# Turned edge blocks of the bands in unused scores columns, two PSUM banks each for middles and sums

## The chip, the core and the metric

The kernel runs on one core of one Trainium2 chip. The metric is device time in microseconds (us) of one launch. Five engines run side by side, each in the order of its own instruction list: TensorE (PE in the profile; its weight loads are listed apart as PEld), VectorE (DVE), ScalarE (ACT), GpSimd (POOL) and SyncE (SP, which issues the DMAs). They hold each other up only through semaphores. TensorE writes its results into PSUM, which has 8 banks; a bank holds 512 fp32 values in each of the 128 partitions. VectorE and ScalarE read them from there.

## What is computed

A two-layer encoder trunk over 1024 tokens of width 1024. In each layer a normalised and modulated input goes through one projection, whose columns feed three groups of attention heads; their outputs are normalised by group, joined, projected back and added to the input; a SwiGLU block follows. Cut to what matters here:

```python
ya = neighborhood_attention(qa, ka, va, rpb_na[l])                  # 4 heads
yb = sliding_window_attention(qb, kb, vb, sink_sw[l], t5_table)     # 6 heads
yc = axial_attention(qc, kc, vc, gq_ax[l], gk_ax[l])                # 6 heads, dense
y = concatenate([rms_norm(ya, ga), rms_norm(yb, gb), rms_norm(yc, gc)], axis=-1)
x = x + gt_a * (y @ w_o[l])
```

For the first two kinds a block of 128 queries sees only three blocks of 128 keys: its own, the one before and the one after. The kernel calls such heads bands (A: the neighbourhood, B: the sliding window).

## The kernel before

**The stream.** The attention of a layer is a list of 64 pairs. A pair is two neighbouring query blocks of one head, so a head has four pairs (p = 0 to 3). Pairs 0 to 23 are the six dense heads (C), 24 to 39 the four heads of A, 40 to 63 the six heads of B. One loop walks over n; in step n work of several pairs is issued, so that each engine finds something ready. While `pin` is on, TensorE, ScalarE and VectorE run in exactly the order in which the code issues. What stands outside (statistics and scales of the group norms, splits of `y` and of weights, the first matmuls of the output projection) is placed freely by a scheduler.

**A step of the bands (n from 24 on), as written.**

1. `divide` for pair n+2: VectorE reciprocal, POOL scales both halves of the probabilities `pr`.
2. `low` for pair n-1: VectorE subtracts the rounded copy from the turned block, `pt<-T` on DVE.
3. `combine` for pair n-3 if its p is odd: VectorE adds the two halves of the head, `y<-pv,cmb`.
4. `scores` for pair n+4: four matmuls into a scores tile (`sA` or `sB`, two banks, columns 0 to 383 of each used), then two VectorE instructions, here called the mins, that add the bias, write `pr` and give the row's extreme.
5. `exps` for pair n+3: two ScalarE exponentials with sums.
6. `turn` for pair n: TensorE transposes the four middle blocks into a tile `T` (`t_tile`, one bank) and the one or two edge blocks (the key blocks outside the pair's own two) into a second such tile `E`, named `T` too in the profile. ScalarE copies both out: `pt<-T` and `edge<-T`.
7. `pv` for pair n-2: four matmuls with the middles, one or two with the edges, into half of a sums bank `pv`; two pairs share a bank.
8. `fold` for pair n-2 if p is odd: ScalarE copies one half, `cmb<-pv`.

**PSUM.** The scores pool `psS` has two tiles of two banks. The remaining four banks are a pool `psT` of three (`PS_T = 3`), from which `T`, `E` and the tiles of the norm statistics (`ps_st`, `ps_r`) are taken in turn, and a pool `psV` of one bank for the sums:

```python
psT_cm, psT = open_pool("psT", bufs=PS_T, space=PSUM)
psV_cm, psV = open_pool("psV", bufs=4 - PS_T, space=PSUM)
```

With one sums bank, the `pv` of an even pair (step n) has to wait for `combine` of the pair before it, which is issued in the same step. `E` of pair n takes the bank that `T` of pair n-1 held, so its transposes wait for `low` of pair n-1, also of the same step.

**After the bands.** From n = 60 no scores are left to issue; the scheduler then places matmuls of the output projection (`ps_o`) between the last turns and sums, with weights split by ScalarE (`whi`) and VectorE (`wlo`).

Of the kernel before, what the change touches and what calls it, by code (L numbers as in the profile page):

```python
# [19 lines left out]
P = 128  # L20
# [7 lines left out]
EPS = 1e-6  # L28
MASKED = 1e30
BIG = 3.0e38  # L30
PS_T = 3

# [53 lines left out]
def trunk(ctx: ExitStack, tc, A, C, out):  # L86
# [19 lines left out]
    def close(cm):  # L106
        cm.__exit__(None, None, None)
# [153 lines left out]
    class Ahead:  # L261


        def __init__(self, gen):
            self.gen, self.have = gen, []
# [592 lines left out]
    for l in range(2):  # L858
# [446 lines left out]
        ap_cm, app = open_pool("apad", side="right")  # L1305
        pad(app, 32)
        at_cm, atp = open_pool("att", side="right")
        psT_cm, psT = open_pool("psT", bufs=PS_T, space=PSUM)
        psV_cm, psV = open_pool("psV", bufs=4 - PS_T, space=PSUM)

        def zA_tile():
            return atp.tile([P, 640], F32, name="zA", tag="zA", bufs=2)
# [19 lines left out]
        def rs_tile():  # L1332
            return atp.tile([P, 8], F32, name="rs", tag="rs", bufs=6)

        def t_tile():
            return psT.tile([P, 4, P], F32, name="T", tag="T")

        def split_pt(T, hi, lo):
            act.copy(hi, T)
# [2 lines left out]
        class Pair:  # L1342

            by_columns = False

            def __init__(self, row, vh, p):
                self.row, self.vh, self.p = row, vh, p
# [9 lines left out]
            def products(self, movs, part):  # L1359
                if part == 0:  # L1360
                    if self.p % 2 == 0:
                        open_pv[0] = psV.tile([P, H], F32, name="pv", tag="V")
                    self.pvt = open_pv[0]
                c0 = (self.p % 2) * 256
                half = (len(movs) + 1) // 2
                for n, (kc, at, mvs) in enumerate(movs):
                    if (n < half) != (part == 0):
                        continue
                    for i, mv in enumerate(mvs):
                        v = vs[:, kc, self.vh, :]  # L1370
# [51 lines left out]
        class PairC(Pair):  # L1422
# [21 lines left out]
            def turn_high(self, c, kb):  # L1444
                if c == kb == 0:
                    self.pt = [[pt_tile() for _ in range(2)] for _ in range(2)]
                cc = slice(c * P, (c + 1) * P)
                T = t_tile()
# [59 lines left out]
        class Band(Pair):  # L1508


            def __init__(self, row, vh, p, q, k, sk=None):
# [7 lines left out]
            def scores(self):  # L1519
                rs, p, sk = self.rs, self.p, self.sk  # L1520
                s, pr = psS.tile([P, 2, 512], F32, name=self.name, tag="S"), self.pr
                for c, (a, b) in enumerate(self.spans):
                    j = 2 * p + c
                    for i in range(2):
                        pe.matmul(
                            s[:, c, a:b], self.q[:, j * P : (j + 1) * P],
                            self.k[i][:, (j - 1) * P + a : (j - 1) * P + b],
                            start=(i == 0), stop=(i == 1),
                        )
                for c, (a, b) in enumerate(self.spans):  # L1530
# [17 lines left out]
            def divide(self):  # L1548
                divide([self.pr[:, c, a:b] for c, (a, b) in enumerate(self.spans)], self.rs)

            def turn(self):
                pr = self.pr
                T, self.pt = t_tile(), [pt_tile() for _ in range(2)]
                for b in range(2):
                    for i in range(2):
                        pe.transpose(
                            T[:, 2 * b + i, :], pr[:, b, (1 - b + i) * P : (2 - b + i) * P], ident
                        )
                edges = [pr[:, 0, 0:P]] * self.left + [pr[:, 1, 2 * P : 3 * P]] * self.right
                E = t_tile()  # L1560
                for i, src in enumerate(edges):
                    pe.transpose(E[:, i, :], src, ident)
                hi, lo = (
                    t[:, 0:2, :].rearrange("p i (c q) -> p c i q", c=2) for t in self.pt
                )
                T = T.rearrange("p (c i) q -> p c i q", c=2)
                act.copy(hi, T)
                e = self.e = atp.tile([P, 2, P], F32, name="edge", tag="edge", bufs=3)
                act.copy(e[:, 0 : len(edges)], E[:, 0 : len(edges)])
                self.low = lambda: sub(lo, T, f32(hi))  # L1570

            def pv(self):
# [142 lines left out]
        for n in range(-AHEAD - 1, N + 3):  # L1715
            ahead = AHEAD if n + AHEAD < NC else AHEAD_B
            begin = range(done, min(n + ahead + 1, N))
            if n < 0:
                begin = range(done, done)
            elif n == 0:  # L1720
                opened(*(pairs[i] for i in range(4)))
                begin = range(3, 4)
                fresh = []
            elif n < NC:
                for i in range(2 if n > 1 else 0):
                    if 0 <= n:
                        pairs[n].turn(i)
                    while unfinished:
                        unfinished.pop(0)()
                    if 2 <= n - 1:  # L1730
                        pairs[n - 1].pv(i)
                    for m in begin:
                        if m < min(made, NC):
                            pairs[m].qk(i)
                for i in range(2 if n == 1 else 0):
                    pairs[begin[0]].qk(i)
                fresh = [pairs[m] for m in begin if NC <= m < made]
                for b in fresh:
                    b.scores()
                    b.exps()  # L1740
                    b.divide()
            else:
                for b in worked:
                    b.divide()
                if NC <= n - 1 < N:
                    pairs[n - 1].low()
                if NC <= n - 3:
                    pairs[n - 3].combine()
                fresh = [pairs[m] for m in begin if m < made]
                for b in fresh:  # L1750
                    b.scores()
                for b in scored:
                    b.exps()
                if n < N:
                    pairs[n].turn()
                if NC <= n - 2 < N:
                    pairs[n - 2].pv()
                    pairs[n - 2].fold()
                elif n == NC:
                    for i in range(2):  # L1760
                        pairs[n - 1].pv(i)
                scored, worked = fresh, scored
# [37 lines left out]
            for end, (chunks, width) in norms.items():  # L1800
                if begins[end] <= m <= end and (m - begins[end]) % 8 == 7 and (n <= NC or m >= NC):
# [9 lines left out]
                    if m == end and end < N - 1:  # L1811

                        def stats(end=end, width=width, n=n, chunks=chunks):
                            r = rstd_cols([gss[end]], width, 8, atp, psT, tag="T", newton=True)

                            def scale():
                                todo = norm_scale(chunks, r, psT, "T", (pool, pool))
# [8 lines left out]
        close(psV_cm)  # L1826
        close(psT_cm)
        close(vs_cm)


# [694 lines left out]
```

## Time and profile before

| | |
|---|---|
| median of 3 runs | 2392.12 us (2391.35 to 2399.88) |
| the profiled execution | 2392.3 us |
| its span, first to last instruction | 2390.5 us |
| granted TensorE clock, mean | 0.995 |
| bands of layer 0, about | 384 to 490 us of the span |
| bands of layer 1, about | 1545 to 1651 us |

All engine instructions are issued by one helper, so they carry one line (L49); they are told apart by engine, operation and tile names (`out<-in`). In a group's row the numbers after the bar are the busy time in us and the mean duration in ns, then the engine's idle time just before these instructions and what ended most of it. In a row of the waits the numbers are the total in us, the count, and the longest. A row of the timeline gives start and duration in us. The second layer runs the same program as the first, 1161 us later.

### The profile page before, as it was taken

What the parts mean: (1) busy time and instruction counts of PE and PEld (TensorE: products, weight loads), DVE (VectorE), ACT (ScalarE), POOL (GpSimd) and SP (SyncE); (2) the same over time, 40 slices, a digit from 0 to 9 for tenths busy, and PEclk for the clock granted to TensorE, in tenths of its full rate; (3) what the DMA queues carried; (4) which work ended last, traced back from release to release, by engine and by line L of the source; (5) the groups of instructions that cost most, each with busy time, mean ns of one, the idle gap of its engine ahead of it and who ended that gap; (6) DMA issues with size and microseconds to landing.
All of it is one profiled execution on the core that took longest, in us unless ns stands there. A gap on an engine that the chain in (4) does not pass through costs nothing. (4 is left out here: it accounts for less than half of the span.)

```text
span 2390.5 us, 33337 instructions
## 1 busy us (share of the span) xinstructions
PE 2333.6 (98%) x11733; PEld 1952.1 (82%) x11733; DVE 1756.9 (73%) x2756; ACT 1185.1 (50%) x2260; POOL 774.2 (32%) x747
## 2 busy tenths in 40 slices
PE   8999999999999999999999999999999999999998
PEld 5787888888788888888887889888878888888886
DVE  6767898977857787596677679987796664537865
ACT  4422788944543333344533158897454333334443
POOL 1440356810244444300035124575005443430001
PEclk9999999999999999999999999999999999999999
DMA  8567416154345344585434861242634443329633
GB/s 280 150 183 226 141 33 176 57 196 131 108 142 180 125 164 149 183 268 179 154 95 117 269 188 28 69 122 74 223 94 132 154 151 106 105 96 292 219 121 110
DMA packets 307415, 357.99 MB, mean 150 GB/s; under 512 B 51996, under 2 KB 223868, under 8 KB 307248
## 3 DMA queue, kind: packets, MB, share of 16 engines
q1 hardware_dynamic: 290752, 346.26, 45.8%
q10 hardware_dynamic: 16128, 9.44, 1.5%
q8 instruction: 92, 1.51, 0.3%
q14 instruction: 75, 0.61, 0.1%
q0 software_dynamic: 368, 0.17, 0.0%
HBM read 270.84 MB, written 88.63 MB: 150 GB/s over the span
## 5 line engine op out<-in xcount | busy, mean ns | idle before, releaser
L49 PE MATMUL ps_d<-wpt 128*128 128x512 f32 x1848 | 423.8, 390 | 1.0 <-ACT wpt L49 0.7
L49 PEld LDWEIGHTS ps_d<-wpt 128*128 128x128 f32 x1848 | 345.7, 188 | 74.4 <-issue 3.0
L49 POOL TENSOR_SCALAR pr<-pr,rs 128x1024 f32<-128x1024 f32 (+2 forms) x248 | 190.5, 784 | 189.2 <-DVE rs L49 171.6
L49 POOL TENSOR_TENSOR sg<-sg,u 128x512 f32<-128x512 f32 x82 | 118.0, 1440 | 348.4 <-ACT sg L49 224.8
L49 PE MATMUL pv<-pt,vs 128*128 128x256 f32 x1088 | 176.0, 296 | 16.3 <-DVE y L49 13.8
L49 DVE TENSOR_TENSOR pt<-T,pt 128x512 fp32r<-128x512 f32 x272 | 177.6, 680 | 7.0 <-ACT pt L49 5.9
L49 ACT CAST wpt<-w 128x512 fp32r<-128x512 f32 x154 | 95.6, 621 | 174.9 <-PE ps_d L49 156.0
L49 ACT CAST pt<-T 128x512 fp32r<-128x512 f32 x272 | 151.7, 586 | 42.2 <-PE T L49 40.5
L49 POOL TENSOR_TENSOR wpt<-ws,wpt 128x512 fp32r<-128x512 f32 x80 | 110.9, 1387 | 181.0 <-ACT wpt L49 133.7
L49 DVE SCALAR_TENSOR_TENSOR acc<-wmt,condT,acc 128x512 f32<-128x512 f32 (+1 forms) x98 | 116.0, 1191 | 72.0 <-DMA wmt<-in_w_mod_dram 71.5
L49 ACT COPY u<-ps_w 128x512 f32<-128x512 f32 x128 | 75.1, 587 | 189.4 <-PE ps_w L49 187.2
L49 DVE TENSOR_TENSOR wpt<-w,wpt 128x512 fp32r<-128x512 f32 x154 | 109.0, 708 | 79.9 <-ACT wpt L49 77.7
L49 PEld LDWEIGHTS pv<-pt,vs 128*128 128x128 f32 x1088 | 142.1, 189 | 29.7 <-DVE y L49 25.4
L49 PE MATMUL T<-identr,pr 128*128 128x128 f32 x1176 | 160.7, 273 | 1.1 <-DVE pt L49 0.6
L49 PEld LDWEIGHTS T<-identr,pr 128*128 128x128 f32 x1176 | 137.8, 140 | 15.6 <-ACT edge L49 1.1
L49 ACT CAST wpt<-ws 128x512 fp32r<-128x512 f32 x176 | 107.8, 622 | 55.3 <-PE ps_w L49 25.4
L49 DVE TENSOR_TENSOR wpt<-graw,wpt 128x512 fp32r<-128x512 f32 x154 | 110.1, 715 | 17.2 <-ACT wpt L49 17.2
L49 ACT CAST wpt<-graw 128x512 fp32r<-128x512 f32 x154 | 95.0, 617 | 53.2 <-DMA graw<-gpd 49.1
L49 DVE TENSOR_TENSOR ws<-wr 128x512 f32<-128x512 f32 x88 | 82.2, 936 | 49.4 <-POOL wpt L49 46.0
L49 DVE TENSOR_TENSOR wpt<-ws,wpt 128x512 fp32r<-128x512 f32 x96 | 81.0, 852 | 49.7 <-ACT wpt L49 49.4
L49 DVE TENSOR_REDUCE rs<-sC 128x1 f32<-128x1024 f32 x88 | 107.2, 1220 | 12.5 <-PE sC L49 11.4
L49 PE MATMUL sC<-qk 128*128 128x512 f32 x384 | 108.5, 406 | 3.7 <-ACT pr L49 3.5
(308 smaller groups left out, 5953.8 us busy)
## 6 DMA issues: line engine op xcount, KB each, us to landing
wr<-in_w_gu_dram SPq DMA_DIRECT2D x92, 512.0 KB, 4.4
gpd<-sg SPq DMA_DIRECT2D x154, 256.0 KB, 4.4
graw<-gpd SPq DMA_DIRECT2D x76, 512.0 KB, 3.5
w<-in_w_down_dram SPq DMA_DIRECT2D x110, 256.0 KB, 4.9
wmt<-in_w_mod_dram SPq DMA_DIRECT2D x48, 512.0 KB, 5.5
qk<-qkd SPq DMA_DIRECT2D x44, 512.0 KB, 7.0
wst<-in_w_o_dram SPq DMA_DIRECT2D x32, 512.0 KB, 4.0
wmt<-in_w_mod_dram SPq DMA_DIRECT2D x64, 256.0 KB, 3.8
```

The costliest lines, as they stand in the source:

```text
L49: ins = op(*args, **kwargs)
```

## The change

Three things are changed in the attention loop.

- The four banks become four pools of one bank, and a small class `Turns` hands them out in a fixed order, separately for each user: in the dense heads 0, 1, 2 for turned blocks and 3 for sums, as before; in the bands 0 and 1 for the middles (and for `ps_st` and `ps_r`), 2 and 3 for the sums; in the last four pairs, where no later scores exist, 0, 1, 1, 0 for middles and edges.
- `scores` is cut into `dots` (the matmuls) and `mins` (the VectorE part). Between them stands `turn_edges`: the edge blocks of pair n are transposed into columns 384 to 511 of the two banks that hold the scores of pair n+4.
- `turn` transposes edges itself only in the last four pairs. The copy `edge` on ScalarE now reads the scores tile.

```diff
-        psT_cm, psT = open_pool("psT", bufs=PS_T, space=PSUM)
-        psV_cm, psV = open_pool("psV", bufs=4 - PS_T, space=PSUM)
+        banks = [open_pool(f"psb{i}", space=PSUM) for i in range(4)]
+
+        class Turns:
+            def __init__(self, order):
+                self.order, self.n = order, 0
+
+            def tile(self, shape, dtype, name, tag=None):
+                b = self.order[self.n % len(self.order)]
+                self.n += 1
+                return banks[b][1].tile(shape, dtype, name=name, tag="b")
+
+        turns_c, turns_b = Turns((0, 1, 2)), Turns((0, 1))
+        turns_e = Turns((0, 1, 1, 0))
+        sums_c, sums_b = Turns((3,)), Turns((2, 3))
...
-                        open_pv[0] = psV.tile([P, H], F32, name="pv", tag="V")
+                        open_pv[0] = self.sums.tile([P, H], F32, name="pv")
...
-            def turn(self):
+            def turn_edges(self, E):
                 pr = self.pr
-                T, self.pt = t_tile(), [pt_tile() for _ in range(2)]
+                edges = [pr[:, 0, 0:P]] * self.left + [pr[:, 1, 2 * P : 3 * P]] * self.right
+                self.E = E[:, 0 : len(edges)]
+                for i, src in enumerate(edges):
+                    pe.transpose(E[:, i, :], src, ident)
+
+            def turn(self, turns, alone):
+                pr = self.pr
+                T, self.pt = t_tile(turns), [pt_tile() for _ in range(2)]
...
-                edges = [pr[:, 0, 0:P]] * self.left + [pr[:, 1, 2 * P : 3 * P]] * self.right
-                E = t_tile()
-                for i, src in enumerate(edges):
-                    pe.transpose(E[:, i, :], src, ident)
+                if alone:
+                    self.turn_edges(t_tile(turns))
...
                 act.copy(hi, T)
                 e = self.e = atp.tile([P, 2, P], F32, name="edge", tag="edge", bufs=3)
-                act.copy(e[:, 0 : len(edges)], E[:, 0 : len(edges)])
+                act.copy(e[:, 0 : self.left + self.right], self.E)
...
                 for b in fresh:
-                    b.scores()
+                    b.dots()
+                for b in fresh:
+                    pairs[n].turn_edges(b.s[:, :, 3 * P : 4 * P])
+                for b in fresh:
+                    b.mins()
                 for b in scored:
                     b.exps()
                 if n < N:
-                    pairs[n].turn()
+                    pairs[n].turn(turns_b if fresh else turns_e, not fresh)
...
-                            r = rstd_cols([gss[end]], width, 8, atp, psT, tag="T", newton=True)
+                            r = rstd_cols([gss[end]], width, 8, atp, turns_b, newton=True)
```

How the instructions move is shown at three places. In brackets stand the engines (or DMA queues) whose semaphores the instruction waits for.

TensorE in a step of B in which a head's first pair is scored and a sums bank is opened, before: scores (`sB`), middles and edge (both `T`), sums (`pv`).

```order
L49 MATMUL sB<-qk 128x256 [waits DMAHW0_49,DVE_49]
L49 MATMUL sB<-qk 128x256
L49 MATMUL sB<-qk 128x384 x2
L49 MATMUL T<-identr,pr 128x128 [waits DVE_49,Pool_49]
L49 MATMUL T<-identr,pr 128x128
L49 MATMUL T<-identr,pr 128x128 [waits Pool_49]
L49 MATMUL T<-identr,pr 128x128
L49 MATMUL T<-identr,pr 128x128 [waits Activation_49]
L49 MATMUL pv<-pt,vs 128x256 [waits DVE_49]
L49 MATMUL pv<-pt,vs 128x256 x3
L49 MATMUL pv<-edge,vs 128x128 x2
```

The same place in the changed kernel:

```order
L48 MATMUL sB<-qk 128x256 [waits DMAHW0_49,PE_49,Activation_49]
L48 MATMUL sB<-qk 128x256
L48 MATMUL sB<-qk 128x384 x2
L48 MATMUL sB<-identr,pr 128x128 [waits Pool_49]
L48 MATMUL T<-identr,pr 128x128 [waits DVE_49]
L48 MATMUL T<-identr,pr 128x128 x3
L48 MATMUL pv<-pt,vs 128x256 x4
L48 MATMUL pv<-edge,vs 128x128 x2
```

The edge stands ahead of the middles and in the scores tile. The scores now wait for ScalarE: their banks are free only when the edge copy of two steps before has read them. The `pv`, which waited for VectorE (`combine`), has no wait any more.

ScalarE in a later step of B, before: two exponentials, middles out, edges out, fold.

```order
L49 ACTIVATE pr,rs<-pr,rs 128x385 [waits DVE_49,Pool_49]
L49 ACTIVATE pr,rs<-pr,rs 128x385 [waits DVE_49]
L49 COPY pt<-T 128x2x2x128 [waits PE_49]
L49 COPY edge<-T 128x128 [waits PE_49]
L49 COPY cmb<-pv 64x512 [waits PE_49,Activation_49]
```

And in the changed kernel:

```order
L48 ACTIVATE pr,rs<-pr,rs 128x385 [waits Pool_49]
L48 ACTIVATE pr,rs<-pr,rs 128x385
L48 COPY pt<-T 128x2x2x128 [waits PE_49]
L48 COPY edge<-sB 128x128 [waits DVE_49,Activation_49]
L48 COPY cmb<-pv 64x512 [waits PE_49,Activation_49]
```

The edge copy waits for VectorE instead of TensorE; the count it waits for is that of the second of the mins of pair n+4, which read the same two banks. The exponentials of the next step, which follow that copy, need no wait for VectorE of their own. Of the work that is not pinned, ScalarE's part of `y_split` (`qk<-y`) stands between such a cast and edge copy in the changed order, behind the edge copy or the exponentials in the old one. VectorE's list is the same in the steps of the bands but for such work, but the mins of pair n+4 now wait for the edge transposes and not only for the scores.

TensorE at n = 60, the first of the last four pairs, before:

```order
L49 MATMUL T<-identr,pr 128x128
L49 MATMUL ps_o<-qk,whi 128x512 [waits Activation_49]
L49 MATMUL T<-identr,pr 128x128 [waits Activation_49]
L49 MATMUL ps_o<-qk,whi 128x512 [waits DVE_49]
L49 MATMUL ps_o<-qk,wlo 128x512 [waits DVE_49]
```

And in the changed kernel:

```order
L48 MATMUL T<-identr,pr 128x128
L48 MATMUL ps_o<-qk,whi 128x512 [waits Activation_49]
L48 MATMUL ps_o<-qk,whi 128x512 [waits PE_49,Activation_49]
L48 MATMUL ps_o<-qk,wlo 128x512 [waits DVE_49]
L48 MATMUL ps_o<-qk,whi 128x512 x2
L48 MATMUL T<-identr,pr 128x128 [waits DVE_49,PE_49]
L48 MATMUL pv<-pt,vs 128x256 x4
```

The one edge of pair 60 waits for VectorE (`low` of pair 59, whose middles held that bank) instead of ScalarE, and has four more `ps_o` ahead of it.

More of the change, by code (lines that the diff above doesn't have):

```diff
@@ L30 @@
 BIG = 3.0e38
-PS_T = 3
 class Engine:
@@ L1333, in rs_tile, with t_tile @@
             return atp.tile([P, 8], F32, name="rs", tag="rs", bufs=6)
-        def t_tile():
-            return psT.tile([P, 4, P], F32, name="T", tag="T")
+        def t_tile(turns):
+            return turns.tile([P, 4, P], F32, name="T")
         def split_pt(T, hi, lo):
@@ L1346, in trunk @@
             by_columns = False
+            sums = sums_c
             def __init__(self, row, vh, p):
@@ L1447, in turn_high @@
                 cc = slice(c * P, (c + 1) * P)
-                T = t_tile()
+                T = t_tile(turns_c)
                 for i in range(4):
@@ L1508, in trunk @@
         class Band(Pair):
+            sums = sums_b
             def __init__(self, row, vh, p, q, k, sk=None):
@@ L1517, in __init__, with dots @@
                 self.spans = [(0 if p > 0 else P, 384), (0, 384 if p < 3 else 256)]
-            def scores(self):
-                rs, p, sk = self.rs, self.p, self.sk
-                s, pr = psS.tile([P, 2, 512], F32, name=self.name, tag="S"), self.pr
+            def dots(self):
+                p = self.p
+                s = self.s = psS.tile([P, 2, 512], F32, name=self.name, tag="S")
                 for c, (a, b) in enumerate(self.spans):
@@ L1529, in scores, with mins @@
                         )
+            def mins(self):
+                s, rs, p, sk, pr = self.s, self.rs, self.p, self.sk, self.pr
                 for c, (a, b) in enumerate(self.spans):
@@ L1750, in trunk @@
                 for b in fresh:
-                    b.scores()
+                    b.dots()
+                for b in fresh:
+                    pairs[n].turn_edges(b.s[:, :, 3 * P : 4 * P])
+                for b in fresh:
+                    b.mins()
                 for b in scored:
@@ L1813, in stats @@
                         def stats(end=end, width=width, n=n, chunks=chunks):
-                            r = rstd_cols([gss[end]], width, 8, atp, psT, tag="T", newton=True)
+                            r = rstd_cols([gss[end]], width, 8, atp, turns_b, newton=True)
                             def scale():
-                                todo = norm_scale(chunks, r, psT, "T", (pool, pool))
+                                todo = norm_scale(chunks, r, turns_b, "b", (pool, pool))
                                 for i, what in enumerate(todo):
@@ L1825, in trunk @@
         pin((pe, act, dve, pool), False)
-        close(psV_cm)
-        close(psT_cm)
+        for cm, _ in banks[::-1]:
+            close(cm)
         close(vs_cm)
```

## The prediction

> **What bounds the kernel now.** I read the page's first part, then its groups, then the bands by stretches of time, then the waits inside them, then the timeline.
>
> ```profile
> span 2390.5 us, 33337 instructions
> PE 2333.6 (98%) x11733; PEld 1952.1 (82%) x11733; DVE 1756.9 (73%) x2756; ACT 1185.1 (50%) x2260; POOL 774.2 (32%) x747
> ...
> L49 PE MATMUL pv<-pt,vs 128*128 128x256 f32 x1088 | 176.0, 296 | 16.3 <-DVE y L49 13.8
> ...
> L49 PEld LDWEIGHTS pv<-pt,vs 128*128 128x128 f32 x1088 | 142.1, 189 | 29.7 <-DVE y L49 25.4
> ```
>
> Over the whole span TensorE looks like the only limit, and its one visible wait is the one that the change takes away: `pv` for `combine` (`DVE y`). But averages hide stages. The stretches show the bands of both layers, cut where the character changes, and one stretch behind:
>
> ```profile
> core 0: us, PE busy (x) PEld busy (x) DVE busy (x) ACT busy (x) POOL busy (x), PEclk, DMA share, GB/s
> 384.00:444.00 60.00, 57.16 (x443) 53.88 (x442) 51.30 (x173) 55.48 (x163) 48.24 (x82) 1.00 0.65 185
> 444.00:474.00 30.00, 26.19 (x201) 24.41 (x199) 29.34 (x90) 29.35 (x81) 23.57 (x40) 1.00 0.03 8
> 474.00:490.00 16.00, 15.14 (x92) 12.44 (x92) 10.40 (x14) 10.60 (x22) 8.25 (x8) 1.00 0.41 133
> 1545.00:1605.00 60.00, 57.11 (x441) 53.85 (x441) 52.00 (x177) 55.74 (x165) 46.59 (x79) 1.00 0.57 158
> 1605.00:1635.00 30.00, 25.81 (x195) 23.65 (x194) 29.34 (x85) 29.32 (x79) 24.65 (x40) 1.00 0.03 8
> 1635.00:1651.00 16.00, 15.54 (x95) 13.09 (x95) 10.32 (x13) 10.50 (x20) 7.54 (x8) 1.00 0.41 132
> 490.00:520.00 30.00, 30.00 (x147) 25.02 (x146) 22.01 (x32) 14.79 (x21) 6.58 (x5) 1.00 0.41 131
> ```
>
> In the first 60 us of the bands ACT is busy for 55.48 of 60, in the next 30 us ACT and DVE both for 29.3 of 30, and there PE is the engine with time to spare. PE is the bound only in the last 16 us and behind them (30.00 of 30.00). So freeing PE can shorten the bands only by what ACT has left: 4.52 + 0.65 us in layer 0, 4.26 + 0.68 in layer 1, together 10.1 us. What is saved there is kept, since PE has no gap behind the bands in which an earlier start could vanish.
>
> ```profile
> PEld pv L49 <- DVE y L49: 11.1, 16, 1.6
> PE pv L49 <- DVE y L49: 6.6, 11, 1.3
> ACT pt L49 <- PE T L49: 3.5, 8, 1.1
> ACT cmb L49 <- PE pv L49: 0.8, 2, 0.5
> PEld T L49 <- ACT edge L49: 0.5, 1, 0.5
> ...
> ACT cmb L49 <- PE pv L49: 0.5, 2, 0.3
> ```
>
> These are the waits of 384 to 490 us (the last row: of 1545 to 1651 us; the other rows read the same there). PE's wait for `combine` is 11.1 us per layer by its weight loads. ACT's waits for PE are only 3.5 + 0.8 us (3.5 + 0.5 in layer 1). They are what a PE that runs ahead can remove.
>
> The Trainium skill's page "Perfetto Trace Analysis", in "Identifying the Most-Contended Engine", says that matmul busy time judges TensorE badly and that the share of weight loads is the better sign. This trace agrees: the same wait is 6.6 us in the matmul rows and 11.1 us in those of the loads, since a matmul's modelled end covers part of a gap; by the one row the wait would be worth 13.2 us in both layers, by the other 22.2.
>
> **The change part by part.** No instruction is added or dropped: the same transposes, copies and matmuls run, at other places. Only waits move.
>
> *Two sums banks.* The `pv` of an even pair no longer waits for `combine` of the same step. PE runs ahead by up to a step, until `T` waits for `low` of two pairs before. What PE gains passes on where ACT waited for PE. The largest case is behind the column sums of a norm, which hold PE for 1.87 us:
>
> ```profile
> 396.93 1.87 PEld L49 LDWEIGHTS ps_st<-onesr,gss 128*128 128x128 f32 x16
> ...
> 400.18 0.59 ACT L49 CAST pt<-T 128x512 fp32r<-128x512 f32 x1 [1.10 <-PE T L49]
> ```
>
> I take all of ACT's waits for PE as gone but the part in the last 16 us, where ACT isn't the bound (about 0.6 us per layer, an estimate): 4.3 + 4.0 - 1.2 = 7.1 us gained. Bounds: 0, and ACT's whole idle time, 10.1.
>
> *Edges in the scores banks: the new wait.* ScalarE's edge copy must now come after both mins of pair n+4 on VectorE. Queued behind it on ACT are `fold`, the next two exponentials and the next `pt<-T`; `combine` and `low` on DVE wait for these in turn. How late it comes is read from where the two stand today. One step of B with a `combine`:
>
> ```profile
> 436.51 0.59 ACT L49 COPY cmb<-pv 64x512 f32<-64x512 f32 x1
> 437.13 0.68 DVE L49 TENSOR_TENSOR y<-pv,cmb 64x512 f32<-64x512 f32 x1 [0.20 <-ACT cmb L49]
> 437.74 0.60 DVE L49 CUSTOM_DVE_ANT_0 pr<-sB,bz,sinkc 128x384 f32<-128x384 f32 x1
> 438.33 0.59 ACT L49 CAST pt<-T 128x512 fp32r<-128x512 f32 x1
> 438.41 0.62 DVE L49 CUSTOM_DVE_ANT_0 pr<-sB,bz,sinkc 128x384 f32<-128x384 f32 x1
> 438.81 0.38 ACT L49 COPY edge<-T 128x256 f32<-128x256 f32 x1
> 438.96 0.08 DVE L49 DVE_READ_ACCUMULATOR2_ANT rs<- 128x1 f32 x1
> ```
>
> The fold ends at 437.10 and `combine` starts 0.03 later; the mins end at 438.96 + 0.08 = 439.04. With a handover of 0.03 the edge copy would start at 439.07 instead of 438.81: 0.26 us late. And this chain closes on itself (fold, combine, mins, edge copy, exponentials, cast, fold), so the delay isn't absorbed. The other step of a head with a `combine`, and one of A:
>
> ```profile
> 433.99 0.08 DVE L49 DVE_READ_ACCUMULATOR2_ANT rs<- 128x1 f32 x1
> 434.02 0.27 ACT L49 COPY edge<-T 128x128 f32<-128x128 f32 x1
> ...
> 394.64 0.07 DVE L49 DVE_READ_ACCUMULATOR2_ANT rs<- 128x1 f32 x1
> 394.80 0.27 ACT L49 COPY edge<-T 128x128 f32<-128x128 f32 x1
> ```
>
> 434.07 + 0.03 against 434.02 is 0.08 us late; in A the mins are done at 394.71, before the copy starts, and it costs nothing. So 0.34 us per head once the mins read `sB`, three heads before 444 us: 1.0 us per layer, 2.0 together.
>
> From 444 us on VectorE has extra work and lags behind ScalarE:
>
> ```profile
> 444.22 0.27 ACT L49 COPY edge<-T 128x128 f32<-128x128 f32 x1
> 444.75 0.08 DVE L49 DVE_READ_ACCUMULATOR2_ANT rs<- 128x1 f32 x1
> ...
> 471.08 0.37 ACT L49 COPY edge<-T 128x256 f32<-128x256 f32 x1
> 471.45 0.08 DVE L49 DVE_READ_ACCUMULATOR2_ANT rs<- 128x1 f32 x1
> ```
>
> Here nine of twelve edge copies start before the mins of their step have ended; these are the first and the last, 0.61 and 0.45 us early, and the nine make 4.7 us. ACT would wait for all of it. But DVE, busy for 29.34 of 30, sets the pace and has the work either way; it loses only what ACT's lateness brings back to it through `low` and `combine`. Bounds 0 and 4.7 us per layer. I take 1.0, nearer to nothing, because DVE is the busier of the two: 2.0 together.
>
> *Edges ahead of the middles, and scores that wait for the edge copy.* Scores of pair n+4 need the copy of step n-2, which in the rows above starts 0.5 us after the cast, with more than a step of PE's work in between. I cost it at nothing; PE's share in that stretch, 26.19 of 30, is the cover. The mins' new wait for the edge transposes falls away likewise when PE is ahead.
>
> *The last four pairs.* They lose a bank, PE is the bound there, and both sides count:
>
> ```profile
> 474.30 0.14 PEld L49 LDWEIGHTS T<-identr,pr 128*128 128x128 f32 x1 [0.54 <-ACT edge L49]
> 474.94 0.66 DVE L49 TENSOR_TENSOR pt<-T,pt 128x512 fp32r<-128x512 f32 x1
> 475.56 0.19 PEld L49 LDWEIGHTS ps_o<-qk,wlo 128*128 128x128 f32 x1
> 481.90 0.53 PEld L49 LDWEIGHTS pv<-pt,vs 128*128 128x128 f32 x4 [0.89 <-DVE y L49]
> ```
>
> The last wait for `combine`, 0.89 us, goes. The edge of pair 60 waits for the `low` that ends at 475.60 instead of starting at 474.30: 1.30 us, of which four `ps_o` moved ahead of it cover 4 x 0.19 = 0.76. Net 0.54 - 0.89 = -0.35 per layer, -0.7 together; bounds -2.9 (both waits, 0.54 and 0.89, gone in both layers) and +2.6 (1.30 uncovered twice, the wait for `combine` replaced by another).
>
> The norm tiles, which now take a turn of two banks instead of three, can hold `T` for the `low` just before it; that was `E`'s wait in every step until now and showed no row of its own above 0.5 us, so I add nothing.
>
> Sum: -7.1 + 2.0 + 2.0 - 0.7 = -3.8 us against the profiled 2392.3 us, which is 0.2 us above the median of the runs: 2388.5 us.
>
> **Rivals.** *Faster by over 0.5%* (12.0 us): the edge copy never holds ACT, ACT closes all its 10.1 us, and the tail gives 2.9: 13.0 us, 2379 us. For it: in A there is no conflict, and free ScalarE work (`qk<-y`) was placed ahead of the edge copies, into the new gaps. Against: ACT would have to be busy without a break, while three engines hand work to each other. The 22.2 us of the weight loads can't come out, as ACT has only 10.1. *Slower*: in the chain fold, combine, mins, edge copy the wait decides. All 4.7 us after 444 and the 1.0 before come onto the path in each layer, the tail adds its 1.30, and ACT's old waits for PE turn into waits for DVE without gain: 2 x 7.0 = 14.0 us, 2406 us. It decides as soon as ACT waits for the mins longer than it waited for PE (4.3 us per layer). For it: DVE and ACT both at 98% in 30 us of each layer, and a step's slack between them is given up. Against: where DVE is the bound, a later ACT costs little.
>
> The Trainium skill speaks for this rival: its page "PSUM — Partial Sum Buffer", in "PSUM bank collisions raise a hardware error", says that two engines must never be on one bank at once, reads by ScalarE against reads by VectorE included, whatever columns they touch. The changed order agrees, with a wait of every edge copy for both mins; no run here shows what happens without it. By that rule alone, with nothing hidden, the result would be the 2406 us above.
>
> *Nothing moves*: PE's wait only changes its name, to `T` for `low` or scores for the edge copy, and ACT goes on as it did, since the rows of ACT's waits for PE came from the norm's column sums, which stay: 2392 us.
>
> **How the numbers follow.** The forecast, 2388.5, has 0.44, nothing moves 0.20, faster 0.21, slower 0.15. The first two lie within 0.5%, which is about what a measurement of this kernel can tell from no change: same 0.64, faster 0.21, slower 0.15. The likeliest case's own range comes from its bounds: 2381 (10.1 + 2.9 - 2.0 = 11.0 us gained) to 2396 (late heads at 4.7 each instead of 1.0: -3.8 + 7.4 = 3.6 us lost). To leave out no more than 2 in 10 the range goes on towards the two other cases: 2377 to 2403.
>
> **What would show it.** In the waits of the same stretches `pv <- DVE y` falls from 11.1 us per layer to below 2, and PE waits for `T` or the scores instead. A new row, ACT `edge` for DVE `pr`, appears: under 3 us per layer if I am right, over 5 if the rival is. ACT's waits for `T` fall from 3.5 to about 1. The end of each layer's bands comes about 2 us earlier. I am wrong if ACT's idle time in the bands grows, or if DVE gains an idle time it doesn't have now.

## The result and the profile after

| | before | after |
|---|---|---|
| median | 2391.43 us (20 runs, 2388.68 to 2399.88) | 2398.41 us (20 runs, 2395.91 to 2402.84) |
| ratio, 95% interval | | 1.0025 (1.0019 to 1.0031) |
| span of the profiled execution | 2390.5 us | 2396.5 us |

The change costs 0.25%, about 6 us (0.0025 x 2391; the two medians lie 7.0 us apart), where 3.8 us less were forecast. By the prediction's bound of 0.5% that is "no change", and it lies in the range; but the sign is wrong, the interval leaves out no difference, and the likeliest case's own range (2381 to 2396) misses it.

First, where. The bands have no fixed ends, so two TensorE groups serve as marks: the first scores of the bands, and the first column sum behind the attention. A row of the view by tile gives the count, the shortest, median and longest duration in ns, then first start and last end. Before, the marks of layer 0 and of layer 1:

```profile
L49 PEld LDWEIGHTS sA<-qk x20: 187/188/192, 378.3 to 383.1; 128*128 128x128 f32 x20
L49 PEld LDWEIGHTS ps_st<-onesr,ssq x8: 188/192/192, 539.8 to 540.7; 128*128 128x128 f32 x8
...
L49 PEld LDWEIGHTS sA<-qk x20: 187/188/193, 1529.5 to 1542.8; 128*128 128x128 f32 x20
L49 PEld LDWEIGHTS ps_st<-onesr,ssq x8: 187/192/192, 1699.5 to 1700.4; 128*128 128x128 f32 x8
```

The same marks after:

```profile
L48 PEld LDWEIGHTS sA<-qk x20: 186/188/192, 378.6 to 383.3; 128*128 128x128 f32 x20
L48 PEld LDWEIGHTS ps_st<-onesr,ssq x8: 187/192/192, 542.8 to 543.7; 128*128 128x128 f32 x8
...
L48 PEld LDWEIGHTS sA<-qk x16: 187/188/192, 1532.4 to 1544.9; 128*128 128x128 f32 x16
L48 PEld LDWEIGHTS ps_st<-onesr,ssq x8: 188/192/192, 1706.2 to 1707.1; 128*128 128x128 f32 x8
```

From mark to mark the first layer takes 161.5 us before and 164.2 after, the second 170.0 and 173.8: 2.7 and 3.8 us more, 6.5 together. That is the whole difference of the two spans (6.0 us): the loss arises between these marks.

The stretches of time, as in the prediction, now read:

```profile
core 0: us, PE busy (x) PEld busy (x) DVE busy (x) ACT busy (x) POOL busy (x), PEclk, DMA share, GB/s
384.00:444.00 60.00, 57.41 (x439) 53.49 (x437) 50.72 (x174) 56.52 (x164) 47.34 (x79) 1.00 0.66 185
444.00:474.00 30.00, 27.85 (x200) 26.23 (x201) 28.12 (x85) 26.67 (x74) 22.11 (x39) 0.94 0.03 8
474.00:490.00 16.00, 12.81 (x75) 9.90 (x74) 12.29 (x20) 10.99 (x24) 9.72 (x10) 1.00 0.31 98
...
1545.00:1605.00 60.00, 57.81 (x434) 54.38 (x432) 51.84 (x171) 55.20 (x157) 46.31 (x77) 0.97 0.58 159
1605.00:1635.00 30.00, 28.07 (x192) 25.98 (x192) 26.68 (x82) 26.19 (x74) 20.91 (x36) 0.89 0.06 14
```

In the 30 us where VectorE and ScalarE had been busy for 29.3, they now have 1.9 to 3.8 us of idle time: 28.12 and 26.67 in layer 0, 26.68 and 26.19 in layer 1. That is what the prediction named as the sign that it is wrong. In the last four pairs (474 to 490) TensorE is idle for 3.2 us of 16, where it was 0.9. The waits of 384 to 490 us say who waits now:

```profile
ACT edge L48 <- DVE rs L48: 3.1, 7, 0.7
PEld sB L48 <- ACT edge L48: 2.8, 6, 0.8
DVE y L48 <- ACT cmb L48: 2.7, 7, 0.9
DVE pt L48 <- ACT pt L48: 2.5, 6, 0.8
ACT pt L48 <- PE T L48: 2.5, 4, 1.1
...
PE T L48 <- DVE isq L48: 1.3, 1, 1.3
PE T L48 <- DVE pt L48: 1.2, 2, 1.1
...
ACT edge L48 <- DVE isq L48: 0.2, 1, 0.2
```

TensorE's wait for `combine` (11.1 us per layer by its weight loads) has no row any more: the second sums bank did what it was made for. The edge copy's wait for the mins is there (3.1 + 0.2 us; 1.9 in layer 1). VectorE waits for ScalarE's fold (2.7 us, before 1.4) and cast (2.5, before 1.3), and ScalarE still waits 2.5 us for middles, and 5.0 us in layer 1, where 1 was forecast. And these middles (`T`) now wait for VectorE, 1.3 and 1.2 us in the matmul rows, where before such waits came to 0.2. The timeline shows one such place, behind the column sum of a norm:

```profile
440.87 1.87 PEld L48 LDWEIGHTS ps_st<-onesr,gss 128*128 128x128 f32 x16
...
442.87 0.17 DVE L48 TENSOR_SCALAR isq<-ps_st 128x8 f32<-128x8 f32 x1 [1.37 <-PE ps_st L48]
443.18 0.75 DVE L48 SCALAR_TENSOR_TENSOR qk<-y,vecs,qk 128x512 fp32r<-128x512 f32 x1
444.00 0.67 DVE L48 TENSOR_TENSOR pt<-T,pt 128x512 fp32r<-128x512 f32 x1
444.78 0.42 PEld L48 LDWEIGHTS T<-identr,pr 128*128 128x128 f32 x4 [1.57 <-issue]
444.81 0.63 PE L48 MATMUL T<-identr,pr 128*128 128x128 f32 x4 [1.30 <-DVE isq L48]
445.48 0.59 ACT L48 CAST pt<-T 128x512 fp32r<-128x512 f32 x1 [1.09 <-PE T L48]
```

The norm tile `ps_st` took the bank whose turn it was, so the next middles fall on the bank that the pair just before still holds. They start at 444.81, when that pair's `low` (`pt<-T` on VectorE, 444.00 + 0.67) has ended; `low` itself stood behind the statistics and a split of `y`. (The profile names the instruction that ended last before; by the program, the transposes need only that `low` has read their bank.) ScalarE stands idle for 1.09 us ahead of its cast.

### The profile page after: what moved, and what is told of

Same layout as the page of the kernel before. It is cut to its first block, busy times and chain, and to the rows that moved or that the text cites. A ratio compares the mean times of both kernels' runs of the same rounds, so it can differ in the third digit from the quotient of the medians.

```text
span 2396.5 us, 33315 instructions
## 1 busy us (share of the span) xinstructions
PE 2339.2 (98%) x11733; PEld 1956.8 (82%) x11733; DVE 1760.7 (73%) x2756; ACT 1188.1 (50%) x2260; POOL 776.9 (32%) x747
## 4 chain that ended last, share of the span: by engine, by line
PE 55%; DVE 4%; issue 4%; ACT 2%; POOL 1%; DMA 1%; SPq 0%; POOLq 0%; ACTq 0%; DVEq 0%
PE ps_w L48 24%; PE ps_d L48 15%; PE ps_o L48 4%; PE ps_ab L48 3%; PE pv L48 2%; PE T L48 2%; PE ps_v L48 2%; PE sC L48 2%; ACT pr L48 1%; PE ps_c L48 1%; DMA graw<-gpd 0%; DVE ws L48 0%; PE sA L48 0%; PE ps_st L48 0%; DVE pt L48 0%
## 5 line engine op out<-in xcount | busy, mean ns | idle before, releaser
L48 PE MATMUL T<-identr,pr 128*128 128x128 f32 x1068 | 152.3, 275 | 7.0 <-POOL pr L48 2.4
L48 PEld LDWEIGHTS T<-identr,pr 128*128 128x128 f32 x1068 | 125.0, 141 | 25.0 <-POOL pr L48 2.9
L48 DVE TENSOR_TENSOR wlo<-wst,whi 128x1024 fp32r<-128x1024 f32 x68 | 88.4, 1302 | 33.3 <-ACT whi L48 28.2
```

Of the source, the lines that this page charges most:

```text
L48: ins = op(*args, **kwargs)
```

## The experiments

All are timed against the kernel before on the same chip. Behind each median stand the ratio to it and, in brackets, the ratio's 95% interval. Differences in us are differences of ratios times 2391.

**Which part costs: edges alone, sums alone, a later copy, the last four pairs.**

Edges alone:

```diff
-        turns_c, turns_b = Turns((0, 1, 2)), Turns((0, 1))
-        turns_e = Turns((0, 1, 1, 0))
-        sums_c, sums_b = Turns((3,)), Turns((2, 3))
+        turns_c, turns_b = Turns((0, 1, 2)), Turns((0, 1, 2))
+        turns_e = turns_b
+        sums_c, sums_b = Turns((3,)), Turns((3,))
```

> Edges stay in the scores banks, but there is one sums bank again and three banks for the middles (in the last four pairs for middles and edges too, as before). Coupling theory (the changed kernel's 7 us come from ScalarE's edge copy waiting for VectorE's mins and the scores waiting for that copy): the loss stays or grows, since the wait of pv for combine is back: 2398 us or more. Tail theory (they come from the last four pairs with only two banks for middles and edges, where TensorE is the bound; there the trace has 1.85 us lost in each layer): 2394.5 us or less, since the tail has its three banks again.

Measured 2399.44 us, 1.0035 (1.0022 to 1.0049). The edges cost 8 us with three banks for middles everywhere, the last four pairs included, so two banks there are not the cause.

Sums alone:

```diff
-                for b in fresh:
-                    pairs[n].turn_edges(b.s[:, :, 3 * P : 4 * P])
...
-                    pairs[n].turn(turns_b if fresh else turns_e, not fresh)
+                    pairs[n].turn(turns_e, True)
```

> Two sums banks are kept, but no edge goes into the scores banks: middles and edges of all pairs share two banks, in the order 0, 1, 1, 0 that the change uses in the last four pairs. Coupling theory: what the edges cost is gone, 2392 us or less, if two banks for middles and edges are enough. Tail theory: the last four pairs are as in the change, so at least 3.7 us of the loss stay, and all other steps now run as the last four do: 2398 us or more.

Measured 2400.73 us, 1.0037 (1.0024 to 1.0049). The number is the one that the tail theory gave, but it doesn't tell the theories apart: two banks for middles and edges together are not enough by themselves. Its waits of 384 to 490 us:

```profile
PE T L48 <- ACT edge L48: 4.9, 8, 3.2
PEld T L48 <- DVE pt L48: 4.9, 8, 1.3
```

The late copy:

```diff
-                act.copy(e[:, 0 : self.left + self.right], self.E)
+                self.out = lambda: act.copy(e[:, 0 : self.left + self.right], self.E)
+                if alone:
+                    self.out()
...
                 for b in scored:
                     b.exps()
+                if NC < n and n - 1 < N - AHEAD_B:
+                    pairs[n - 1].out()
```

> The edge copy moves on ScalarE behind the two exponentials of the next step, which wait for the same mins anyway, so it never waits for VectorE of its own; banks as in the change. Coupling theory: the copy's wait (2 to 3 us per layer) and what it passes on go, 2393 to 2395 us; the scores' wait for the copy may get longer, which takes part of it back. Tail theory: 2397 us or more, since the last four pairs are as in the change.

Measured 2390.37 us, 0.9998 (0.9989 to 1.0007): the whole loss is gone, more than expected.

The last four pairs on three banks:

```diff
-        turns_e = Turns((0, 1, 1, 0))
-        sums_c, sums_b = Turns((3,)), Turns((2, 3))
+        turns_e = Turns((0, 1, 2))
+        sums_c, sums_b = Turns((3,)), Turns((2, 3) * 9 + (3, 3))
```

> As the change, but the last four pairs get three banks for middles and edges and one for their sums, as in the kernel before. Tail theory: 1.85 us per layer come back, 2394.5 us or less. Coupling theory: 2397 to 2399 us, as the change.

Measured 2400.98 us, 1.0035 (1.0022 to 1.0048). Together with the late copy:

> The late edge copy and the three banks in the last four pairs together. With the late copy alone TensorE still loses 1.2 us in the last four pairs of each layer; if that is due to their two banks, this kernel is at 2388 us, below the kernel before (2391.7). If the banks of the last four pairs don't matter, it stays at the 2390.4 us of the late copy alone, or above.

2393.51 us, 1.0007 (0.9999 to 1.0016). Twice no gain: the tail theory falls.

**Is it the wait or the place?** The kernel before with the same late copy (edges in their own banks):

> The kernel before with the same move of the edge copy (behind the next step's exponentials), edges in banks of their own. Waiting theory (what the late copy saved in the changed kernel is the copy's wait for the mins): nothing to save here, 2391 to 2394 us. Place theory (the copy is better placed there whatever it waits for, since it no longer holds up the fold and what follows): the same 8 us are saved here, 2384 us.

Measured 2400.39 us, 1.0035 (1.0022 to 1.0049). Neither theory gave this. The place theory falls, and more: by itself the late place costs 8 us. Its waits of 384 to 490 us:

```profile
ACT cmb L49 <- PE pv L49: 4.8, 14, 0.6
```

The fold, now right behind the cast, waits 4.8 us for the sums, and 4.4 in layer 1; before it was 0.8 and 0.5. The copy used to fill that time.

Edges in the earlier scores tile:

```diff
-                for b in fresh:
-                    pairs[n].turn_edges(b.s[:, :, 3 * P : 4 * P])
...
-                    pairs[n].turn(turns_b if fresh else turns_e, not fresh)
+                    E = pairs[n + 3].s[:, :, 3 * P : 4 * P] if fresh else None
+                    pairs[n].turn(turns_b if fresh else turns_e, E)
```

> The edges of pair n are turned, behind its middles, into the scores tile of pair n+3, whose mins were done a step earlier, and not of pair n+4; the copy keeps its place. Waiting theory: the copy doesn't wait for mins any more, 2390 to 2394 us; the scores of the next step now wait for it, which may cost more. Place theory: 2397 us or more, since the copy still stands ahead of the fold.

Measured 2407.32 us, 1.0066 (1.0053 to 1.0078). By its number that is the place theory's, which the run above has refuted; the rows give another reason. The wait for the mins is gone, but the scores of the next step now wait for the copy (384 to 490 us):

```profile
PEld sB L48 <- ACT edge L48: 9.6, 19, 1.6
...
PEld sA L48 <- ACT edge L48: 3.6, 6, 1.6
```

Fold first (the copy, as `out` above, behind `fold` in the same step):

> As the change, but the edge copy stands behind the fold of the same step; it waits for the same mins. Waiting theory: ScalarE still waits, only with the fold ahead of it, and the exponentials wait behind it: 2395 to 2399 us. Place theory: the fold and combine are free of it, 2390 to 2393 us.

Measured 2394.15 us, 1.0013 (1.0005 to 1.0022): half of the loss is gone (2.9 us, give or take 2.5) though the copy waits as long as in the change (2.2 + 0.5 us of 384 to 490). So that half came from the fold queued behind the copy, and from what waits for the fold.

**The wait by itself**, added to the kernel before, and its control, the same instruction with nothing new to wait for (`pairs[n]` in place of `pairs[n + 4]`):

```diff
-                act.copy(e[:, 0 : len(edges)], E[:, 0 : len(edges)])
+                    act.activation(e, E, AF.Copy, scale=by.rs[:, 1:2])
...
-                    pairs[n].turn()
+                    pairs[n].turn(pairs[n + 4] if fresh else None)
```

> The kernel before, with one thing added: the edge copy is multiplied by the extreme that the second of the mins of pair n+4 writes (the edges come out scaled, so the output is another), which makes ScalarE wait for both mins exactly where the change does. Banks and order are as before. Waiting theory: this wait by itself costs most of the change's 7 us: 2396 to 2400 us. If the loss comes from the scores banks held longer or from edges ahead of middles, the wait costs little: 2391 to 2393 us.

> The control to the wait alone: the same multiplication, by the extreme of pair n itself, which has been there for steps, so nothing new is waited for (the edges come out scaled, so the output is another). Both theories: as before but for some 0.05 us per copy, 2391 to 2394 us.

The wait alone: 2406.05 us, 1.0058 (1.0046 to 1.0070). The control: 2397.49 us, 1.0025 (1.0015 to 1.0034). The difference, 0.0033, is the wait: 7.9 us, give or take 3.6 (the two half-widths, 0.0012 and 0.00095, as the root of the sum of their squares). Its rows, of 384 to 490 us and of 1545 to 1651 us:

```profile
ACT edge L49 <- DVE rs L49: 4.0, 12, 0.8
...
ACT edge L49 <- DVE isq L49: 0.9, 1, 0.9
...
ACT edge L49 <- DVE rs L49: 2.5, 9, 0.8
...
ACT edge L49 <- DVE isq L49: 0.9, 1, 0.9
...
ACT edge L49 <- DVE rstd L49: 0.3, 1, 0.3
```

ScalarE waits 8.6 us, and the kernel is 7.9 us longer. The control is telling too; the groups by form (busy us, mean ns of one, idle us before), of the kernel before and of the control:

```profile
L49 ACT COPY edge<-T 128x256 f32<-128x256 f32 x40 | 15.0, 375 | 0.0
L49 ACT COPY edge<-T 128x128 f32<-128x128 f32 x40 | 10.9, 272 | 0.0
```

```profile
L49 ACT ACTIVATE edge<-T,rs 128x256 f32<-128x256 f32 x36 | 17.2, 479 | 0.0
L49 ACT ACTIVATE edge<-T,rs 128x128 f32<-128x128 f32 x36 | 13.5, 375 | 0.0
```

72 copies became 104 or 103 ns longer each, twice the 50 ns expected: 7.5 us of ScalarE work, and the kernel is 6.0 us longer (3.6 to 8.1 by the interval). So most of ScalarE's time counts in the bands.

**What the second sums bank is worth.** The late copy with one sums bank (the late copy's edit and that of the edges alone):

> The late edge copy with edges in the scores banks, but one sums bank and three banks for middles. If the second sums bank gains something once the copy waits for nothing of its own, this is slower than the 2390.4 us of the late copy with two sums banks by up to 7 us: 2393 to 2397. If its wait only changes its name (nothing moves), it is the same within 1.5 us: 2389 to 2392.

Measured 2398.23 us, 1.0030 (1.0020 to 1.0040), against 0.9998 with two: the second bank is worth 0.0032, 7.7 us (give or take 3.2), once no copy waits for mins. With the copy in its place it is worth 0.0010 (edges alone against the change), 2.4 us, which the intervals (1.0022 to 1.0049, 1.0019 to 1.0031) don't tell from nothing.

**What eats that gain with the late copy?** First, middles ahead of the scores on TensorE:

> The late edge copy, and on TensorE the middles of pair n ahead of the scores of pair n+4, so that what ScalarE needs next is not queued behind scores that wait for its own edge copy (8.3 us of such waits per layer in the late copy's trace). If that wait is what eats the gain of two sums banks: 2385 to 2388 us. If VectorE and ScalarE set the pace anyway: 2389 to 2392 us.

Measured 2400.8 us, 1.0037 (1.0024 to 1.0051). Scores, and so mins, now come later by four transposes; this order costs 9 us against the late copy, which neither theory gave. Then edges turned at the end of the step, behind the sums:

> The late edge copy, and the edges of pair n are turned at the end of the step, behind the sums, into the same scores tile: so the mins of pair n+4 wait for their scores alone, and the edge transposes wait for the mins. If the mins' wait for the edges (and GpSimd's scale) is what eats the gain of two sums banks: 2384 to 2388 us. If the scores' wait for the copy eats it: 2390 to 2393 us, as the late copy alone (2390.4).

Measured 2403.13 us, 1.0047 (1.0033 to 1.0060); TensorE now waits for the mins with the next scores behind it (384 to 474 us):

```profile
PEld sB L48 <- DVE rs L48: 9.3, 18, 1.3
...
PEld sA L48 <- DVE rs L48: 4.4, 8, 1.6
```

> The same with three banks for middles and edges in the last four pairs. If the last four pairs lose anything to two banks once nothing else is late: 1 to 3 us below the late edges with two. If not: the same within 1 us, or above, as when this was tried with the late copy alone (2393.5 against 2390.4).

Measured 2404.37 us, 1.0049 (1.0036 to 1.0061): again nothing from the last four pairs.

**The norm tiles.** In the change:

```diff
-                            r = rstd_cols([gss[end]], width, 8, atp, turns_b, newton=True)
+                            r = rstd_cols([gss[end]], width, 8, atp, sums_b, newton=True)
...
-                                todo = norm_scale(chunks, r, turns_b, "b", (pool, pool))
+                                todo = norm_scale(chunks, r, sums_b, "b", (pool, pool))
```

> As the change, but the norm tiles take their turn on the sums banks and not on those of the middles. If the norm tiles on the middles' banks cost what they seem to (one wait of 1.1 to 1.3 us per norm that shows one, one or two per layer): 2394 to 2396 us. If sums or other work wait in their place: 2397 to 2400 us, as the change (2398.4).

Measured 2392.17 us, 1.0001 (0.9992 to 1.0010). More than expected: the whole loss is gone, 0.0024 or 5.7 us (give or take 2.6), with the edge copy untouched. The marks of this kernel:

```profile
L48 PEld LDWEIGHTS sA<-qk x24: 187/188/192, 377.0 to 385.0; 128*128 128x128 f32 x24
L48 PEld LDWEIGHTS ps_st<-onesr,ssq x8: 188/192/192, 538.5 to 539.4; 128*128 128x128 f32 x8
...
L48 PEld LDWEIGHTS sA<-qk x20: 187/188/193, 1530.2 to 1543.2; 128*128 128x128 f32 x20
L48 PEld LDWEIGHTS ps_st<-onesr,ssq x8: 188/192/192, 1700.4 to 1701.2; 128*128 128x128 f32 x8
```

161.5 and 170.2 us, the 161.5 and 170.0 of before. The last four pairs of layer 0, with the change's own two banks, also read as before (15.14 of 16 us there), so TensorE's 3.2 idle us in the change were lateness carried in:

```profile
474.00:490.00 16.00, 14.94 (x94) 12.61 (x93) 10.60 (x13) 10.30 (x20) 6.45 (x8) 1.00 0.44 133
```

ScalarE's waits for middles in the change, of 384 to 475 us and of 1545 to 1636 us:

```profile
ACT pt L48 <- PE T L48: 2.3, 3, 1.1
...
ACT pt L48 <- PE T L48: 4.8, 5, 1.5
```

With the norm tiles on the sums banks neither stretch has such a row: 7.1 us are gone, though the edge copy still waits for VectorE (2.0 + 1.2 us, and 1.4 + 1.2 in layer 1). And the place shown above:

```profile
437.49 1.87 PEld L48 LDWEIGHTS ps_st<-onesr,gss 128*128 128x128 f32 x16
...
439.80 0.75 DVE L48 SCALAR_TENSOR_TENSOR qk<-y,vecs,qk 128x512 fp32r<-128x512 f32 x1
439.98 0.47 PEld L48 LDWEIGHTS T<-identr,pr 128*128 128x128 f32 x4
...
440.61 0.67 DVE L48 TENSOR_TENSOR pt<-T,pt 128x512 fp32r<-128x512 f32 x1
```

The middles start at 439.98, before the `low` of the pair ahead (440.61), with the same split of `y` in front of that `low`. The sums pay a little: `pv` for `combine` is back with 2.1 us in that layer.

With the late copy, norm tiles on the sums banks too:

> The late edge copy with the norm tiles on the sums banks. If the norm tiles cost something there: 2387 to 2389 us. If not: 2389.5 to 2392 us, as the late copy alone (2390.4).

2392.07 us, 1.0003 (0.9994 to 1.0011): no further gain. The copy between the two exponentials of the next step, alone and with the norm tiles moved:

> The edge copy stands between the two exponentials of the next step: still behind nothing that comes later than the mins, but some 0.8 us earlier than in the late copy, so that the scores wait less for it. If that wait is what eats the gain: 2385 to 2388 us. If VectorE sets the pace in the bands (29.5 of 30 us busy from 444 us on with the late copy): 2389 to 2392 us. If the copy waits for the second of the mins again: 2393 us or more.

> Both: the copy between the exponentials and the norm tiles on the sums banks. If both waits count: 2384 to 2387 us; if only one does, as that one alone; if neither: 2389 to 2392 us.

2391.63 us, 0.9997 (0.9988 to 1.0006), and 2388.19 us, 0.9990 (0.9981 to 0.9999). The last is the fastest median of all, 2.4 us under the kernel before and some 8 under the change (0.0035). Against before its interval only just leaves out no difference, and it is the best of several tries.

## Why the prediction was wrong

- **What bounds the bands: right.** ScalarE, then ScalarE with VectorE. The control showed it directly: 7.5 us of added ScalarE work, 6 us of time.
- **Two sums banks, -7.1 us: right in kind and size, where it can act.** 7.7 us with the late copy. In the change itself the gain is spent.
- **The edge copy's wait, +4.0: too small.** Alone in the kernel before it costs 7.9 us; in the change ScalarE waits 5.2 us (3.1 + 0.2 + 1.9). The part in doubt, from 444 us on, was well priced: 1.0 per layer, against 1.2 and 1.0 in the change and 1.4 and 1.5 in the wait alone. The part before 444 us was not: again 1.0 per layer, from three heads of B, against 2.1 and 0.9 in the change and 3.5 and 2.4 in the wait alone. Of the 2.1 us, 0.63 + 0.74 + 0.40 stand before 402 us, in steps that score a head of A, where one step had been read and the wait taken to cost nothing. The sign that was named (under 3 us per layer if right, over 5 if the rival is) reads 3.3 and 1.9.
- **The norm tiles, 0: this step failed.** The prediction saw the mechanism: they "can hold `T` for the `low` just before it; that was `E`'s wait in every step until now and showed no row of its own above 0.5 us, so I add nothing". Moving them to the sums banks gives back 5.7 us. The error was to read the price off the edges. Behind a late `E` stood the edge copy; behind late middles stand the cast, on the engine that bounds, and on TensorE's own queue the sums and the scores for the next mins. A norm draws three tiles, two norms per layer fall into the bands: twelve turns in all, about 0.5 us each on the mean. That these tiles cost the 5.7 us is shown by moving nothing else; how much of it is the bank's wait itself, and how much the slower TensorE clock behind it (last section), is not.
- **The last four pairs, -0.7:** with three banks nothing measurable came back, three times. A term of about nothing is not contradicted.
- **Edges ahead of middles and scores waiting for the copy, 0:** not priced apart. A copy some 0.8 us earlier (between the exponentials against behind them) changed nothing, 0.9997 against 0.9998; but with one step less of room (the earlier tile) the kernel is 15.8 us slower than before. So the cover that the prediction counted on was needed, and about enough.

With measured sizes the sum is -7.7 + 5.2 + 5.7 = +3.2, or +5.9 with the wait's 7.9, against +6.0 measured. It is not a strict sum: the late copy alone and the moved norm tiles alone each bring back the 6 us, and both together no more. Nor does moving the norm tiles give the 3.8 us that were forecast without them, but the time of before (0.2 us over it, -1.9 to +2.4 by the interval). For the late copy a reason is likely: the place costs 8 us of its own in the kernel before, by the fold's wait. With it `low` also came right behind the statistics at the place looked at. How much of each is in its 0.9998 stays open, and so does how much the free work (splits, norms), which the scheduler places anew in every variant, adds to single results.

*The rivals.* "Slower" had the right engine pair but a price of 14 us, in which no sums gain was left; the wait costs about half of that, and the gain exists. That rival leaned on the Trainium skill's page "PSUM — Partial Sum Buffer" ("PSUM bank collisions raise a hardware error"), by which two engines must not be on one bank at once. In the change every edge copy from a scores bank is ordered behind VectorE's reads of it; no run shows what happens without. "Nothing moves" was nearest in time, but its mechanism is refuted by the second bank's 7.7 us.

## What to carry to other kernels

When a round-robin of buffers shrinks, list every other user that draws from it: an occasional tile shifts the turn and makes the next urgent tile wait for the newest holder, not the oldest. Price that by what stands behind the waiting instruction, not by what the same wait cost a less urgent one. Count a new wait of the engine that bounds a stage in full (8.6 us of waits cost 7.9 here), read it off every kind of step and not off one, and test a suspected wait by adding it alone to the old kernel, beside a control that has the instruction without the wait.

## What the runs showed of the hardware

In the change's profile the granted TensorE clock falls to half behind the column sums of three of the four norms in the bands. The stretch ahead of the middles shown above, the stretch behind it, and one in layer 1 behind the same norm:

```profile
443.00:445.00 2.00, 0.70 (x6) 0.43 (x5) 1.82 (x7) 1.36 (x5) 0.82 (x2) 1.00 0.20 72
445.00:449.00 4.00, 4.00 (x21) 3.90 (x20) 2.82 (x12) 3.07 (x8) 1.64 (x5) 0.57 0.00 0
1606.00:1612.00 6.00, 5.39 (x23) 4.82 (x23) 4.58 (x17) 4.48 (x12) 2.46 (x6) 0.50 0.09 28
```

In stretches of 10 or 20 us the change has 0.83 in 440 to 450, 1560 to 1570 (0.50 in 1562 to 1564) and 1600 to 1620 us. The kernel before and the one with the moved norm tiles have 1.00 in all three; before has a dip elsewhere:

```profile
230.00:260.00 30.00, 27.36 (x145) 22.68 (x144) 21.94 (x32) 14.65 (x26) 6.66 (x6) 0.94 0.43 132
```

Of ScalarE's 7.1 us of waits for middles in the change, 4.9 us (0.79 + 0.97 + 0.68 + 1.49 + 0.96) end inside such a dip or within 1 us behind it, so the slow clock may be a good part of what the norm tiles cost. It need not cost: the kernel with the copy between the exponentials also has 0.83 in 440 to 450 and 1600 to 1620 us, and is as fast as before.

Many runs don't average this out. The mean clock of the change's 20 runs is 0.9934, that of the 11 with the moved norm tiles 0.9953, and that of the 33 runs of before beside these 0.997. Where the means are equal, 0.993 to 0.995, the change takes 2397.9 us (15 runs) and the kernel with the moved norm tiles 2392.5 us (5 runs), so the lower mean alone doesn't make the difference; where in a run the dips lie, a mean doesn't tell. For the late copy (0.996 to 0.998 in all its runs) that comparison can't be made.

Also unexpected: a ScalarE copy of 128 or 256 columns takes 103 or 104 ns longer when it scales by a value per row (375 against 272 ns, and 479 against 375 ns).
